# Merging the recurrence branch first, and letting another simulation set the order of the whole kernel

## Chip, cores and metric

One core of a Trainium2 chip. The metric is the device time of one execution, in microseconds (us), as the median of several runs. Engines are named as in the profile: PE is TensorE's matmul side and PEld its weight loads, DVE is VectorE, ACT ScalarE, POOL GpSimd, SP SyncE.

## The reference

The model takes 512 tokens of width 1024 through two blocks in float32. The first block mixes tokens in three branches (four heads of gated linear attention, GLA; a short convolution; eight heads of sliding-window attention), adds them with sigmoid gates, projects, and applies a gated feed-forward layer. The second block is applied twice, with its own weights for each layer. Its mixer has two branches: attention in which every query sees only the 128 keys that an index network scored highest, and a recurrence (HGRN) of four heads. The two are merged and projected:

```python
z = rmsnorm(h) @ w_in            # q, k, v, index inputs, recurrence inputs, gates
y_attn = dsa_attention(q, k, v, qi, ki, wi) @ w_attn_o
y_rec  = hgrn(f, i, ...) @ w_hgrn_o
merged = sigmoid(gate_a) * y_attn + sigmoid(gate_b) * y_rec
h = h + merged @ w_out
h = h + feed_forward(rmsnorm(h))
```

(The names are shortened; the sum over the two branches can be taken in either order.)

## The kernel before

All activations are kept with features on the partitions, as tiles of 128 x 512 (512 is the number of tokens); attention and recurrence use tiles with tokens on the partitions, NT = 4 token tiles of 128. The width 1024 makes KD = 8 feature tiles. Every large product is split into high and low parts, so that one product of a weight tile and an activation tile is three matmuls: in `project`, L193 (low weight, high activation), L194 (high weight, low activation) and L195 (high, high), each 128 x 512; in `project_tokens`, L168 to L170. A weight tile comes by DMA on SP's queue (`wraw`, three buffers), ACT casts it to `whi` (L149), and POOL or DVE subtracts it to `wlo` (L152).

The stages run in this order: a setup; the first mix (`first_mix`: GLA heads, window attention `swa`, convolution, merge of the three); the first feed-forward layer; then for each of two layers `second_mix` and `second_ffn`. `second_mix` calls `dsa` for the attention branch, then makes four recurrence heads (`hgrn_head`, which ends in `recurrence`), and merges both branches with `merge`.

In `dsa`, the string `ORDER` sets the order in which the steps are written: `x` and `X` make and rotate the index inputs, `1` to `3` are `select` (four score matmuls L874, then sixteen rounds of DVE's L885 maximum and L886 replacement), `k` and `K` make and rotate the keys, `q` and `Q` the queries (one `Q` for each block of 128 queries), `v` the values, `h` the recurrence's values, and `a` to `d` are the four blocks of queries, `attend(0)` to `attend(3)`, with one to four key blocks each. The rotations scale `aro` on DVE (L825) and transpose it on PE (L239).

A block has eight heads, each a chain: QK on PE (L925), bias and minimum on DVE (L927), exponential on ACT (L929), transposes on PE (L933), copy on ACT (L935), PV on PE (L937). After eight heads come reciprocal, scaling to `aon`, four transposes (L239) and the split into `yah` and `yal`, which the output projection of the attention branch reads. A recurrence head starts with L474, climbs seven levels in which DVE, POOL and PE take turns (L485 to L511, POOL's last step L515), and ends with state products (L397, L405, L407), an inverse square root on DVE (L229 to L233), `ron` (L415), its transposes (L239) and the split into `yhh` and `yhl`.

`merge(W, X, WO, y, acc, ahead, last)` makes `ahead` gates first, then for each of the eight output tiles one more gate, the output projection of the branch, and their product; the first branch that is merged has `acc=None` and keeps its products as the accumulator. A gate reads only the layer's input X; an output projection reads the branch's `y`, so it needs all of that branch.

PSUM has four banks for `project` ("mm"), two for the attention and two for the recurrence ("at"). Buffers of SBUF are pools: "t" (32 tiles), "i" (8), "g" (5, gates) and others.

Each engine executes its own queue in order. What order that is, the framework's scheduler decides when the kernel is built: it walks through the program and places instructions by their dependences, buffers, priorities (`tc.high_priority()` for weight loads and evictions) and its own estimate of durations. Work of the recurrence heads, gates and projections is thus placed between the steps of the attention heads, where it has no dependence on them.

Of the kernel before, what the change touches and what calls it, by code (L numbers as in the profile page):

```python
# [21 lines left out]
KD = 8  # L22
KF = 22
WARM = 12
ORDER = "xhX123kKqvQaQbQcQd"
EPS = 1e-6
NEG = -1e30
UNSEEN = -2e38
# [42 lines left out]
class Builder:  # L71
# [602 lines left out]
        self.nc.scalar.activation(g, g, AF.Tanh, scale=0.5)  # L674
        return g

    def merge(self, W, X, WO, y, acc, ahead, last):
        nc = self.nc
        G = [self.gate(W[m], X) for m in range(ahead)]
        out = []  # L680
        for m in range(KD):
            if m + ahead < KD:
                G.append(self.gate(W[m + ahead], X))
            g = G[m] if acc else self.t("acc")
            ps = self.project(WO[m], y)
            with self.tc.high_priority():
                nc.vector.scalar_tensor_tensor(g, G[m], 1.0, ps, op0=OP.add, op1=OP.mult)
            if acc:
                eng = nc.vector if last and m + ahead >= KD else nc.gpsimd
                if last and m + ahead == KD:  # L690
                    self.lows = [nc.gpsimd]
                eng.tensor_tensor(acc[m], acc[m], g, op=OP.add)
                g = acc[m]
            out.append(self.split(g, "mg") if last else g)
        return out
# [132 lines left out]
    def dsa(self, l, X):  # L828
# [61 lines left out]
        def inputs(j, name):  # L890
            got[name] = self.attention_inputs(A["w_tok"][l, j], X, name)
# [23 lines left out]
        def attend(i):  # L915
# [27 lines left out]
            for m in range(4):  # L943
# [3 lines left out]
                     q=lambda: inputs(1, "aq"), Q=rotate_query, v=values, h=gated_values)  # L947
        for c in ORDER:
            if c in steps:
# [7 lines left out]
    def second_mix(self, l, X):  # L957
        nc, A = self.nc, self.A
        W = A["w_in2"][l]
        it = iter(range(W.shape[0]))  # L960
        proj = lambda: self.project(W[next(it)], X)

        with self.on("a"):
            yattn = self.dsa(l, X)
        if self.pending:
            self.settle()
        hv = self.hv
        yh = []
        for hd in range(4):
            F = self.scaled(proj(), "hf", self.i)  # L970
            k = self.i("hk")
            nc.scalar.activation(k, F, AF.Sigmoid, scale=-1.0)
            nc.scalar.activation(F, F, AF.Sigmoid)
            if l:
                nc.gpsimd.tensor_scalar(k, k, self.om[:, hd:hd + 1], None, op0=OP.mult)
                nc.vector.tensor_scalar(F, F, self.om[:, hd:hd + 1], self.lb[:, hd:hd + 1], op0=OP.mult, op1=OP.add)
            q = self.silu2(proj(), "hq")
            v = [a[:, hd * P:(hd + 1) * P] for a in hv]
            g = self.silu2(proj(), "hg")
            yh.append(self.hgrn_head(F, q, k, v, g, self.half[:, 4 + l:5 + l], "yh"))  # L980

        acc = self.merge(A["w_gate2"][l, 0], X, A["w_po"][l, 0], yattn, None, 2, False)
        return self.merge(A["w_gate2"][l, 1], X, A["w_po"][l, 1], yh, acc, 4, True)

    def build(self, out):
        nc, A = self.nc, self.A
# [118 lines left out]
```

## Time and profile before

| | us |
|---|---|
| median of 3 runs | 2586.61 (2585.37 to 2587.36) |
| profiled run, its own time | 2592.11 |
| span of the profiled run | 2590.3 |
| PE busy | 2504.4 |
| DVE busy | 1362.4 |
| ACT busy | 1011.7 |
| POOL busy | 769.8 |

The span is the time between the first and the last instruction of one profiled execution; its mean granted clock of TensorE was 0.99. A window gives, for a stretch of this span, how long each engine was busy; the stretch less the busy time of an engine is its idle time. In a timeline row the first number is the start from the beginning of the span, the second the duration; `<-` stands between what is written and what is read, and a bracket at the end tells idle time of that engine just before, and what ended it. Matmuls overlap, so the rows of several matmuls in a row start closer together than one lasts.

### The profile page before, as it was taken

Reading aid. Unit: us, or ns where it says so; the run is one execution under the profiler, and the core shown is the slowest. Engines: PE = TensorE matmul, PEld = TensorE weight load, DVE = VectorE, ACT = ScalarE, POOL = GpSimd, SP = SyncE. Lnnn points to the kernel's source line nnn. Section 1 sums busy time; section 2 is a strip of 40 time slices with the busy share of each in tenths; the row PEclk is TensorE's granted clock in tenths of the full one; section 3 lists DMA queues with packets and bytes.
Section 4 is the critical chain, followed back from the end, with each engine's and each line's share of the span. In section 5 each row is a group of like instructions: output and inputs, shape, how many; then the busy total and the mean of one; then the engine's idle time right before and its main releaser. Section 6 shows DMA issues by size and latency. Waiting matters only on the chain.

```text
span 2590.3 us, 31616 instructions
## 1 busy us (share of the span) xinstructions
PE 2504.4 (97%) x11742; PEld 2047.2 (79%) x11742; DVE 1362.4 (53%) x2568; ACT 1011.7 (39%) x1830; POOL 769.8 (30%) x676
## 2 busy tenths in 40 slices
PE   9999999999999998899999999999798999999999
PEld 7877888888888766777888888887677788888887
DVE  4675222477764677765244444336877523444432
ACT  5633333444443344453343333334355333433322
POOL 4234334511101333643361110013465335211100
PEclk9999999999999999999999999999899999999999
DMA  4112233322233222111332223332211123222233
GB/s 136 58 60 82 87 97 98 102 98 98 97 95 96 76 74 73 42 37 59 94 99 98 97 94 95 94 98 66 73 42 40 34 96 101 96 94 96 97 108 88
DMA packets 67434, 217.66 MB, mean 84 GB/s; under 512 B 7744, under 2 KB 8640, under 8 KB 67280
## 3 DMA queue, kind: packets, MB, share of 16 engines
q1 hardware_dynamic: 67280, 215.65, 26.1%
q8 instruction: 92, 1.51, 0.2%
q14 instruction: 62, 0.51, 0.1%
HBM read 213.52 MB, written 2.10 MB: 83 GB/s over the span
## 4 chain that ended last, share of the span: by engine, by line
PE 80%; DVE 14%; POOL 3%; issue 2%; ACT 1%; DMA 0%; SPq 0%; DVEq 0%; POOLq 0%; ACTq 0%
PE mm L194 23%; PE mm L195 23%; PE mm L193 23%; DVE score L886 2%; DVE m L885 2%; PE at L925 1%; PE at L937 1%; PE at L239 1%; DVE wlo L152 1%; POOL hG L495 1%; PE mm L169 1%; PE mm L170 1%; PE mm L168 1%; DVE rsq_w L231 1%; PE at L933 1%
## 5 line engine op out<-in xcount | busy, mean ns | idle before, releaser
L149 ACT CAST whi<-wraw 128x512 fp32r<-128x512 f32 (+3 forms) x824 | 502.3, 610 | 1139.9 <-PE mm L195 950.4
L193 PE MATMUL mm<-xh,wlo 128*128 128x512 f32 x1920 | 759.0, 395 | 0.0
L194 PE MATMUL mm<-xl,whi 128*128 128x512 f32 x1920 | 758.2, 395 | 0.0
L195 PE MATMUL mm<-xh,whi 128*128 128x512 f32 x1920 | 755.5, 393 | 0.0
L152 DVE TENSOR_TENSOR wlo<-wraw,whi 128x512 fp32r<-128x512 f32 (+1 forms) x529 | 385.2, 728 | 458.5 <-ACT whi L149 455.4
L152 POOL TENSOR_TENSOR wlo<-wraw,whi 128x512 fp32r<-128x512 f32 (+2 forms) x295 | 381.4, 1293 | 760.5 <-ACT whi L149 689.6
L195 PEld LDWEIGHTS mm<-xh,whi 128*128 128x128 f32 x1920 | 361.8, 188 | 74.5 <-issue 1.9
L194 PEld LDWEIGHTS mm<-xl,whi 128*128 128x128 f32 x1920 | 361.9, 188 | 73.5 <-issue 1.7
L193 PEld LDWEIGHTS mm<-xh,wlo 128*128 128x128 f32 x1920 | 361.8, 188 | 72.9 <-issue 1.2
L193 PE MATMUL mm<-acth,wlo 128*128 128x512 f32 x528 | 205.4, 389 | 0.0
L194 PE MATMUL mm<-actl,whi 128*128 128x512 f32 x528 | 205.4, 389 | 0.0
L195 PE MATMUL mm<-acth,whi 128*128 128x512 f32 x528 | 205.4, 389 | 0.0
L733 POOL TENSOR_TENSOR fg<-fg,rstd 128x512 f32<-128x512 f32 x44 | 56.7, 1289 | 425.6 <-ACT fg L732 425.6
L168 PE MATMUL mm<-wlo,xh 128*128 128x512 f32 (+2 forms) x384 | 147.0, 383 | 17.3 <-POOL wlo L152 9.2
L169 PE MATMUL mm<-whi,xl 128*128 128x512 f32 (+2 forms) x384 | 145.2, 378 | 0.2 <-DVE xl L288 0.2
L170 PE MATMUL mm<-whi,xh 128*128 128x512 f32 (+2 forms) x384 | 145.1, 379 | 0.0
L202 DVE TENSOR_TENSOR gate<-mm,rstd 128x512 f32<-128x512 f32 x56 | 38.7, 691 | 165.2 <-PE mm L195 164.3
L277 POOL TENSOR_TENSOR acc<-acc,sq 128x512 f32<-128x512 f32 x39 | 58.9, 1509 | 199.2 <-ACT sq L274 198.3
L194 PEld LDWEIGHTS mm<-actl,whi 128*128 128x128 f32 x528 | 99.1, 188 | 20.8
L193 PEld LDWEIGHTS mm<-acth,wlo 128*128 128x128 f32 x528 | 99.1, 188 | 20.6
L195 PEld LDWEIGHTS mm<-acth,whi 128*128 128x128 f32 x528 | 99.1, 188 | 20.4
L168 PEld LDWEIGHTS mm<-wlo,xh 128*128 128x128 f32 x384 | 73.4, 191 | 36.1 <-POOL wlo L152 11.7
(352 smaller groups left out, 3333.1 us busy)
## 6 DMA issues: line engine op xcount, KB each, us to landing
wraw<-in_w_ffn_in SPq DMA_DIRECT2D x88, 512.0 KB, 3.3
wraw<-in_w_gate SPq DMA_DIRECT2D x56, 512.0 KB, 3.3
wraw<-in_w_in SPq DMA_DIRECT2D x52, 512.0 KB, 3.3
wraw<-in_w_up SPq DMA_DIRECT2D x44, 512.0 KB, 3.2
wraw<-in_w_tok SPq DMA_DIRECT2D x32, 512.0 KB, 3.2
wraw<-in_w_ffn_out SPq DMA_DIRECT2D x32, 512.0 KB, 3.6
wraw<-in_w_down SPq DMA_DIRECT2D x16, 512.0 KB, 3.6
wraw<-in_w_po SPq DMA_DIRECT2D x32, 256.0 KB, 2.6
```

The lines of the kernel that those rows point to most:

```text
L149: nc.scalar.copy(wh, raw[:, k:k + m, :])
L152: eng.tensor_tensor(wl, raw[:, k:k + m, :], wh.bitcast(F32), op=OP.subtract)
L168: nc.tensor.matmul(ps[t][:, 0:w], xh, wl, start=i == 0, stop=False)
L169: nc.tensor.matmul(ps[t][:, 0:w], xl, wh, start=False, stop=False)
L170: nc.tensor.matmul(ps[t][:, 0:w], xh, wh, start=False, stop=i == KD - 1)
L193: nc.tensor.matmul(ps, wl, xh, start=i == 0, stop=False)
L194: nc.tensor.matmul(ps, wh, xl, start=False, stop=False)
L195: nc.tensor.matmul(ps, wh, xh, start=False, stop=i == n - 1)
L277: (nc.vector if d % 2 and len(acc) > 1 else nc.gpsimd).tensor_tensor(a, a, sq, op=OP.add)
L733: nc.gpsimd.tensor_tensor(g, g, self.rstd, op=OP.mult)
L885: nc.vector.max(m8, sc[:, 0:w])
L886: nc.vector.match_replace(sc[:, 0:w], m8, sc[:, 0:w], TAKEN)
```

## The change

Four things change. In `ORDER`, two query rotations stand ahead of the first block in place of one, and the rotations for the last two blocks stand ahead of the block before, so that no rotation stands between the last two blocks. `second_mix` merges the recurrence branch first (two gates ahead) and the attention branch second (four gates ahead, as the last). `merge` gets a parameter for the pool of its accumulator, and the recurrence merge, now first, takes it from pool "i". And the program is built with `schedule_with_timeline_sim=True`: the scheduler then takes the times by which it places instructions from the toolchain's other simulation. That holds for all stages, not only for `second_mix`.

```diff
-ORDER = "xhX123kKqvQaQbQcQd"
+ORDER = "xhX123kKqvQQaQbQcd"
...
-    def merge(self, W, X, WO, y, acc, ahead, last):
+    def merge(self, W, X, WO, y, acc, ahead, last, alloc=None):
...
-            g = G[m] if acc else self.t("acc")
+            g = G[m] if acc else (alloc or self.t)("acc")
...
-        acc = self.merge(A["w_gate2"][l, 0], X, A["w_po"][l, 0], yattn, None, 2, False)
-        return self.merge(A["w_gate2"][l, 1], X, A["w_po"][l, 1], yh, acc, 4, True)
+        acc = self.merge(A["w_gate2"][l, 1], X, A["w_po"][l, 1], yh, None, 2, False, self.i)
+        return self.merge(A["w_gate2"][l, 0], X, A["w_po"][l, 0], yattn, acc, 4, True)
...
-    with tile.TileContext(nc) as tc:
+    with tile.TileContext(nc, schedule_with_timeline_sim=True) as tc:
```

The instructions stay the same in number on PE (10973), DVE (2474), POOL (681) and SP (470); ACT has 1734 instead of 1736. Their order changes on every engine. Four places of it follow; a number behind a name tells tiles of one name apart.

PE, the end of block d in layer 0, before. From the QK of the last head on, L193 to L195 with `xh` and `xl` are projections of a gate.

```order
L925 MATMUL at_8900<-kT_7952,qT_8780 128x512
L239 MATMUL at_9973<-csts_77,ron_9971 128x128 x4
L195 MATMUL mm_10023<-xh_6470,whi_10026 128x512
L193 MATMUL mm_10023<-xh_6579,wlo_10027 128x512
L194 MATMUL mm_10023<-xl_6580,whi_10026 128x512
L195 MATMUL mm_10023<-xh_6579,whi_10026 128x512
L193 MATMUL mm_10023<-xh_6688,wlo_10027 128x512
L194 MATMUL mm_10023<-xl_6689,whi_10026 128x512
L933 MATMUL at_8905<-csts_77,aL_8902 128x128 x4
L195 MATMUL mm_10023<-xh_6688,whi_10026 128x512
L193 MATMUL mm_10023<-xh_6797,wlo_10031 128x512
L194 MATMUL mm_10023<-xl_6798,whi_10030 128x512
```

The same place in the changed kernel: the last two heads and what follows.

```order
L925 MATMUL at<-kT,qT 128x512
L933 MATMUL at<-csts,aL 128x128 x4
L937 MATMUL at<-av,aPT 128x64 x4
L925 MATMUL at<-kT,qT 128x512
L933 MATMUL at<-csts,aL 128x128 x4
L937 MATMUL at<-av,aPT 128x64 x4
L239 MATMUL at<-csts,aon 128x128 x4
L193 MATMUL mm<-yah,wlo 128x512
L193 MATMUL mm<-xh,wlo 128x512
```

The gate's matmuls are gone from between the steps of a head; the same three rows (L925, L933, L937) stand six times in a row up to here, and in layer 1 five times. After the transposes of `aon` comes the first output projection of the attention branch (`yah`).

PE, the start of the fourth recurrence head in layer 0, before: L474 starts it, L488 and L509 are its levels.

```order
L925 MATMUL at_8820<-kT_7950,qT_8779 128x512
L474 MATMUL at_9845<-hq_9798,hk_9760 128x128 x4
L488 MATMUL at_9855<-lvx_9852,ones_78 128x256
L193 MATMUL mm_9985<-xh_6363,wlo_9989 128x512
L194 MATMUL mm_9985<-xl_6364,whi_9988 128x512
L195 MATMUL mm_9985<-xh_6363,whi_9988 128x512
L933 MATMUL at_8825<-csts_77,aL_8822 128x128 x4
L193 MATMUL mm_9985<-xh_6470,wlo_9989 128x512
L194 MATMUL mm_9985<-xl_6471,whi_9988 128x512
L195 MATMUL mm_9985<-xh_6470,whi_9988 128x512
L193 MATMUL mm_9985<-xh_6579,wlo_9989 128x512
L937 MATMUL at_8785<-av_8195,aPT_8830 128x64
```

In the changed kernel, a little further on in the fourth head: L509 and L464 are levels, L239 with `hG` is the transposes that follow them.

```order
L925 MATMUL at<-kT,qT 128x384
L509 MATMUL at<-lvx 112x64 x4
L509 MATMUL at<-lvx 96x64 x4
L933 MATMUL at<-csts,aL 128x128 x3
L464 MATMUL at<-lvx 64x64 x4
L937 MATMUL at<-av,aPT 128x64 x3
L925 MATMUL at<-kT,qT 128x384
L239 MATMUL at<-csts,hG 128x128 x4
L397 MATMUL at<-hv,rklT 128x128 x3
L405 MATMUL at<-hv,AT 128x128 x2
L933 MATMUL at<-csts,aL 128x128 x3
L407 MATMUL at<-rS,hf 128x128
```

Matmuls of gates stood between the levels; now only attention heads of three key blocks do. Ahead of these rows, three output sums of the recurrence merge (`yhh`) are each open on a bank, and each takes its next products when a recurrence head ends.

DVE, the key rotation in layer 0, before: L885 and L886 are rounds of the selections with three (128x384) key blocks, `aro` is what the rotation gives.

```order
L885 MAX m_7704<-score 128x8
L233 SCALAR_TENSOR_TENSOR rsq_y<-rsq_w,rsq_y 128x32
L886 MATCH_REPLACE score<-m_7704,score 128x384
L825 TENSOR_TENSOR aro<-aro,rsq_y 128x512
L885 MAX m_7707<-score 128x8
L825 TENSOR_TENSOR aro<-aro,rsq_y 128x512
L886 MATCH_REPLACE score<-m_7707,score 128x384
L825 TENSOR_TENSOR aro<-aro,rsq_y 128x512
L885 MAX m_7710<-score 128x8
L825 TENSOR_TENSOR aro<-aro,rsq_y 128x512
L886 MATCH_REPLACE score<-m_7710,score 128x384
L885 MAX m_7713<-score 128x8
```

And in the changed kernel:

```order
L233 SCALAR_TENSOR_TENSOR rsq_y<-rsq_w,rsq_y 128x32
L886 MATCH_REPLACE score<-m_7642,score 128x256
L886 MATCH_REPLACE score<-m_7668,score 128x384
L231 TENSOR_TENSOR rsq_w<-akss,rsq_y 128x32
L887 TENSOR_SCALAR score<-score 128x256
L885 MAX m_7671<-score 128x8
L232 SCALAR_TENSOR_TENSOR rsq_w<-rsq_w,rsq_y 128x32
L886 MATCH_REPLACE score<-m_7671,score 128x384
L233 SCALAR_TENSOR_TENSOR rsq_y<-rsq_w,rsq_y 128x32
L885 MAX m_7674<-score 128x8
L825 TENSOR_TENSOR aro<-aro,rsq_y 128x512 x4
L886 MATCH_REPLACE score<-m_7674,score 128x384
```

The four steps on `aro` stand together, earlier among the selection's rounds: ahead of the first, since the first selection's scores were complete, are 37 rows of L885 and L886 instead of 58. On PE, 100 matmuls of 128 x 512 stand between the last score matmul of that selection and the first key transposes instead of 152.

PE, the end of the attention and GLA heads of the first mix, in the changed kernel (L397 to L407 are state products of the last GLA head, L239 with `ron` its transposes):

```order
L397 MATMUL at<-gv,rklT 128x128 x3
L405 MATMUL at<-gv,AT 128x128 x2
L407 MATMUL at<-rS,rE 128x128
L405 MATMUL at<-gv,AT 128x128
L407 MATMUL at<-rS,rE 128x128
L405 MATMUL at<-gv,AT 128x128
L407 MATMUL at<-rS,rE 128x128
L239 MATMUL at<-csts,ron 128x128 x4
L193 MATMUL mm<-xh,wlo 128x512
```

Before, the same products of the last GLA head stood among projections of the convolution:

```order
L397 MATMUL at<-gv,rklT 128x128 x3
L405 MATMUL at<-gv,AT 128x128 x2
L194 MATMUL mm<-xl,whi 128x512
L407 MATMUL at<-rS,rE 128x128
L405 MATMUL at<-gv,AT 128x128
L407 MATMUL at<-rS,rE 128x128
L405 MATMUL at<-gv,AT 128x128
L407 MATMUL at<-rS,rE 128x128
L195 MATMUL mm<-xh,whi 128x512
L193 MATMUL mm<-xh,wlo 128x512
L194 MATMUL mm<-xl,whi 128x512
L195 MATMUL mm<-xh,whi 128x512
```

In the changed kernel no 128 x 512 matmul stands beside the last window block and the last GLA head; the projections of the convolution and all that the merge needs follow in one row.

## Rows read from the trace of the kernel before

**Rows 1.** The page: busy time and instructions of each engine; the chain by engine.

```profile
PE 2504.4 (97%) x11742; PEld 2047.2 (79%) x11742; DVE 1362.4 (53%) x2568; ACT 1011.7 (39%) x1830; POOL 769.8 (30%) x676
...
PE 80%; DVE 14%; POOL 3%; issue 2%; ACT 1%; DMA 0%; SPq 0%; DVEq 0%; POOLq 0%; ACTq 0%
```

**Rows 2.** Windows: stretch, length, busy us (count) of five engines, clock, DMA share, GB/s.

```profile
0.00:30.00 30.00, 24.22 (x97) 19.74 (x97) 18.95 (x30) 15.87 (x28) 14.07 (x13) 0.94 0.59 193
30.00:220.00 190.00, 180.75 (x1015) 149.26 (x1016) 114.91 (x317) 93.31 (x211) 62.98 (x56) 1.00 0.20 64
525.00:870.00 345.00, 345.00 (x1524) 285.67 (x1523) 234.35 (x319) 152.14 (x242) 47.46 (x34) 1.00 0.30 96
870.00:1010.00 140.00, 123.12 (x555) 97.02 (x554) 108.93 (x264) 53.12 (x110) 55.44 (x53) 0.96 0.22 72
1010.00:1212.00 202.00, 185.92 (x1084) 147.90 (x1083) 143.90 (x324) 97.92 (x201) 96.70 (x105) 1.00 0.14 44
1725.00:1860.00 135.00, 120.17 (x534) 94.82 (x533) 97.55 (x234) 51.34 (x107) 53.85 (x52) 0.94 0.22 73
1860.00:2062.00 202.00, 186.62 (x1047) 148.84 (x1046) 141.11 (x321) 95.19 (x197) 100.20 (x107) 0.95 0.13 40
```

**Rows 3.** Timeline, one head of block d: start, us, engine, line; other rows left out.

```profile
1188.28 1.08 PE L925 MATMUL at<-kT,qT 128*128 128x512 f32 x2
...
1189.40 0.69 DVE L927 CUSTOM_DVE_ANT_0 aL<-at,score 128x512 f32<-128x512 f32 x1 [0.29 <-PE at L925]
...
1190.19 0.72 ACT L929 ACTIVATE aL<-aL,anm 128x512 f32<-128x512 f32 x1 [2.22 <-DVE rsq_w L231]
...
1191.06 0.66 PE L933 MATMUL at<-csts,aL 128*128 128x128 f32 x4
...
1191.81 0.59 ACT L935 COPY aPT<-at 128x512 f32<-128x512 f32 x1 [0.18 <-PE at L933]
...
1192.48 1.07 PE L937 MATMUL at<-av,aPT 128*128 128x64 f32 x8
...
1193.39 1.08 PE L925 MATMUL at<-kT,qT 128*128 128x512 f32 x2
```

**Rows 4.** Timeline of DVE and POOL, and a window: one recurrence head.

```profile
1165.21 0.42 DVE L485 TENSOR_TENSOR lvx<-hf,hq 128x256 f32<-128x256 f32 x1
...
1179.04 1.54 POOL L515 TENSOR_TENSOR hG<-hG,hk 128x512 f32<-128x512 f32 x1
...
1193.26 0.69 DVE L415 TENSOR_TENSOR ron<-at,rsq_y 128x512 f32<-128x512 f32 x1
...
1165.50:1194.30 28.80, 27.95 (x182) 22.10 (x181) 23.34 (x52) 9.86 (x20) 14.76 (x16) 1.00 0.08 24
```

**Rows 5.** Timeline at the key rotation of layer 0.

```profile
979.08 1.26 DVE L825 TENSOR_TENSOR aro<-aro,rsq_y 128x512 f32<-128x512 f32 x1
...
980.40 0.90 PE L239 MATMUL at<-csts,aro 128*128 128x128 f32 x3 [8.27 <-DVE aro L825]
```

**Rows 6.** Groups by line on DVE, selection with three key blocks: busy, mean ns, idle.

```profile
L885 DVE MAX8 m<-score 128x8 f32<-128x384 f32 x32 | 17.7, 553 | 0.3
L886 DVE MATCH_REPLACE8 score<-m,score 128x384 f32<-128x384 f32 x32 | 17.3, 540 | 0.0
```

**Rows 7.** Timeline of PE in the first mix.

```profile
133.84 0.61 PE L582 MATMUL at<-csts,sL 128*128 128x128 f32 x4
...
135.22 1.01 PE L588 MATMUL at<-skv,sPT 128*128 128x64 f32 x8
...
211.64 0.39 PE L407 MATMUL at<-rS,rE 128*128 128x128 f32 x2
...
216.89 0.66 PE L239 MATMUL at<-csts,ron 128*128 128x128 f32 x4 [0.28 <-DVE ron L415]
```

**Rows 8.** Windows after the key wait and between the first heads.

```profile
976.20:986.40 10.20, 6.00 (x20) 4.95 (x21) 10.17 (x25) 2.94 (x13) 3.60 (x3) 0.50 0.16 54
1016.90:1023.10 6.20, 3.99 (x18) 2.77 (x19) 4.41 (x11) 3.00 (x6) 0.45 (x1) 1.00 0.00 0
```

## The prediction

> **What bounds the kernel now.** I read the engine line of the page first: PE is busy for 2504.4 of 2590.3 us, so 85.9 us is left in which it has nothing at all, and the chain that ends last is PE for 80% and DVE for 14% [rows 1]. So TensorE bounds the kernel, and a change of order can only win or lose PE's idle time, its slow clock, or both. Next I read the windows by stage, to see where that idle time lies. The feed-forward stretch 525 to 870 has none, and its 1524 matmuls of 345.00 us give 0.2264 us for one 128x512 matmul in a dense row; I call such a one a wide matmul, and use it as the unit of fill. The idle time is window less PE busy: 9.25 us in the first mix (30 to 220), 16.9 in the tokens and keys of layer 0 (870 to 1010), 16.1 in its attention and recurrence (1010 to 1212), 14.8 and 15.4 in the same two stretches of layer 1 [rows 2]. That is 72 of the 85.9, and all the places that the change reorders.
>
> Then the timeline of one attention head with four key blocks, to see what a head costs when nothing fills it [rows 3]. QK starts at 1188.28 and ends at 1189.36; the transposes (L933) start only at 1191.06, after DVE's bias and minimum and ACT's exponential: 1.70 us. They end at 1191.72 and PV (L937) starts at 1192.48, after ACT's copy: 0.76 us. The next QK starts at 1193.39, so the head takes 5.11 us, of which 2.46 us must be filled by other matmuls. In this head twelve wide matmuls stood there (12 x 0.2264 = 2.72 us), so PE never stopped.
>
> Doing the same for a recurrence head: its first DVE step (L485) is at 1165.21, POOL's last level step (L515) ends at 1180.58, and `ron` (L415) is at 1193.26, 28.05 us in all; in 1165.50 to 1194.30 PE was busy for 27.95 of 28.80 us [rows 4]. So the head ran behind full cover, and its own chain is 28 us at most. The level part, 15.4 us of POOL and DVE taking turns, hardly shortens; the 12.7 us after it hold some waits behind other heads, and I estimate 24 us for the chain by itself.
>
> Of TensorE the Trainium skill (Trainium Kernel Development and Optimization, Reading a trace) says that matmul busy time is a bad measure of headroom and weight-load busy a good one. By that measure the dense stretch stands at 285.67 / 345.00 = 82.8% [rows 2] against 2047.2 / 2590.3 = 79.0% for the whole [rows 1], an estimate of 118 us to win at most in place of 86; the sum below does not use it.
>
> **The change part by part.** The instruction counts of PE, DVE, POOL and SP stay what they were, and ACT has two table loads fewer; everything is order.
>
> *Merge order.* Before, only recurrence projections and two gates could run under the attention heads, since the merges began with the attention's output. Now the recurrence merge (its gates and output projections) and four attention gates need no attention output, so they can run there. Counting the wide matmuls in the new order between one QK and the next over the 32 heads of a layer, there are 672 where there were 311. That is more fill than is needed, but it is spent early: the first ten heads and those about the end of block c and the start of block d have 19 to 70 each, where about 12 do. The last six heads of layer 0 and the last five of layer 1 have none (first pair of excerpts). Each such head loses the 2.46 us of [rows 3]: 6 x 2.46 = 14.8, and 5 x 2.46 = 12.3. After the last PV come reciprocal, scaling, transposes and the split before the first `yah` product; only a single gate stands ready, so I add 2.2 us (0.76 and 1.5, the size of one such DVE and ACT pair in [rows 3]). Tails: 17.0 and 14.5 us.
>
> *The middle.* From the 13th to the 20th head there are only 24 wide matmuls (layer 0) and 21 (layer 1), because three of the four PSUM banks for projections hold output sums of the recurrence merge that wait for `yh` of the later recurrence heads. The third and fourth recurrence heads lie there. From L474 to the transposes of `ron` the new order puts 30 and 9 wide matmuls on PE: 6.8 and 2.0 us. Taking the 29 wide matmuls of the head in [rows 4] from its 27.95 us leaves 21.4, which hold five full-width attention heads of 5.11 - 2.46 = 2.65 us, so about 8 to 9 us for the recurrence's own matmuls. The four or so narrower heads beside each (two and three key blocks, estimates 1.3 and 1.8 us) make about 21 and 18 us of PE work. Against a chain of 24 to 28 us that leaves 9 to 17 us idle in the two heads together. PE takes its queue in order, so a wait for one chain also holds up the other; but the fill before it runs densely. I take 12 us per layer, with 4 and 18 as bounds.
>
> With 1 us for the heads that are nearly covered, layer 0 has 17.0 + 12 + 1 = 30 us of idle time in place of 16.1, **+13.9**; layer 1 has 14.5 + 12 + 1 = 27.5 in place of 15.4, **+12.1**.
>
> *Tokens and keys.* Before, PE waited 8.27 us at 980.40 for `aro` [rows 5]: DVE works through the selections (L885, L886) ahead of the key rotation. In the new order 37 of these stand between the first selection's end and the first `aro` instead of 58 (third pair of excerpts): 21 x 0.547 = 11.5 us less DVE work [rows 6]. But PE comes earlier too: 100 wide token matmuls instead of 152 lie between the last score matmul of that selection and the key transposes, 52 x 0.2264 = 11.8 us less. So the wait stays within a few us of 8. It isn't free behind it: two queries are rotated before the first block now, with 30 such DVE steps ahead instead of 24 (+3.3 us, plus the second rotation's own products of some 1 us each, as in [rows 5]) and 9 wide matmuls fewer (-2.0). I put a new wait of 4 to 5 us there, and 3 to 4 us saved at the keys and at the norm's broadcast ahead of them, which now has more token matmuls beside it. Net **+1** per layer, bounds -8 (the wait at the keys goes) and +6 (both waits stand).
>
> *First mix.* The whole program is scheduled anew, so the first mix moves too. Its last window block and last GLA head now run with no wide matmul beside them, while more than a thousand stand behind in one row (fourth pair); before, there was fill to the end. What this costs: from the last state product (ends 212.03) to the transposes of `ron` (216.89) 4.9 us; four transposes-copy-PV steps, each with the 0.77 us from 134.45 to 135.22, 3.1 us [rows 7]; eight score reductions ahead of the first exponential, some 4 us by the 0.69 us of [rows 3] less overlap; 1 us for the rest: 13 us. Against that most of the 9.25 us of [rows 2] goes, since the stages ahead are filled. **+4**, bounds -4 and +10.
>
> *Start.* Two mask casts move ahead of two splits on DVE in the first 30 us, where PE is idle for 5.8 [rows 2]: **+1**, bounds -1 and +3.
>
> *Clock.* After the wait of 8.27 us at the keys, the granted clock of 976.20 to 986.40 is 0.50, which is 1.2 GHz; yet in 1016.90 to 1023.10, where PE is busy 3.99 of 6.20 us, it stays at 1.00 [rows 8]. So gaps of 1 to 2 us with heads between them kept the full clock here, and one long wait did not. The bare heads are of the first kind; they go on for longer, however. I allow **+3** for two or three short stretches. The Trainium skill (TensorE: Matmul & The Clock Gate, A second HAM failure mode: psum-queue depth-cycling) says that PE idling briefly between matmul groups often enough makes the clock oscillate, at a cost to throughput. [rows 8] shows no drop in the shorter stretch; a rival below takes the other side.
>
> The merges, feed-forward stages and norms had no idle time and their rows stay as they were: 0, because wide matmuls cover every load there.
>
> **Sum.** 1 + 4 + 2 x 1 + 13.9 + 12.1 + 3 = +36 us. The profiled run took 2592.11 us (span 2590.3, and 1.8 around it), 5.5 above the median of the runs; 2592.1 + 36 = 2628.1 there, and 2628.1 - 5.5 = **2622.6** as a median; I say 2622.
>
> **Rivals.**
> 1. *DVE is what matters, and it is freed.* If the new order brings DVE's results so much earlier that the key wait goes in both layers (8.27 us and about 3 us for the 6.00 busy us at half clock [rows 5, 8], so -11.3 each in place of +1) and that the recurrence chains in the middle take 20 us or less (12 us each to 0), the sum is 36 - 2 x 12.3 - 2 x 12 = -12.6: about 2574. It decides once the key wait is under 2 us and both late recurrence heads take less than their PE work. For it: DVE is busy 108.93 of 140 and 143.90 of 202 us there [rows 2]. Against it: the levels of a recurrence head are 15.4 us of POOL and DVE in turns whatever the order [rows 4], and the bare heads cost 2.46 each in any case. Chance 0.18.
> 2. *The clock falls in the bare stretches.* All three PE steps of a bare head are on its chain; at 1.2 GHz their 2.65 us double, +2.65 for each of eleven heads, 29 us, and 3 to 6 more in the first mix: about 2655. For it: the 0.50 after the key wait. Against it: the 1.00 at 1016.90 [rows 8]. Chance 0.17.
> 3. *It does nothing that counts.* The order differs from end to end, but idle time moves from one place to another and the sum stays within 5 us, because the middle is covered (4 us) and the first mix wins 4: about 2587 to 2592. Chance 0.09.
>
> **How the numbers follow.** The forecast, 2597 to 2645, has 0.56. A measurement here can tell about 0.2% (5 us) from no change. Slower by more: 0.56 + 0.17 = 0.73; within: 0.09; faster by more: 0.18. The range leaves out about one in ten at each side: 2572, just beyond rival 1, to 2656, at rival 2.
>
> **What would show it.** In the changed kernel the last six and five heads of block d should come 5.1 us apart with PE about half busy; the third and fourth recurrence heads 24 to 28 us long with several us of PE waiting; a PE wait of 5 us or more both at the keys and at the first query; some 13 us of PE idle just ahead of the convolution's projections; and merges as dense as before. I am wrong if the bare heads come closer than 4.5 us, if the middle shows PE dense, or if the key waits vanish.

## The result, and the profile after

The changed kernel takes 2674.19 us (median; 2670.45 to 2675.81) against 2586.99 us for the kernel before in the same runs: a ratio of 1.0335, with a 95% interval of 1.0322 to 1.0348. It is 87 us slower. The forecast was 2622 us, with a range up to 2656: the sign was right and the size far too small.

The profiled execution has a span of 2672.2 us. The page's busy times and the chain by engine, as in [rows 1]:

```profile
PE 2543.9 (95%) x11742; PEld 2086.8 (78%) x11742; DVE 1374.0 (51%) x2568; ACT 1008.4 (38%) x1828; POOL 780.0 (29%) x676
...
PE 83%; DVE 10%; issue 3%; ACT 2%; POOL 1%; DMA 1%; SPq 0%; DVEq 0%; POOLq 0%; ACTq 0%
```

PE executes the same 11742 instructions, yet it is busy 39.5 us longer than in [rows 1] (2543.9 against 2504.4), and idle 42.4 us longer (2672.2 - 2543.9 = 128.3 against 85.9). The two make up the 81.9 us between the spans. The mean granted clock fell from 0.990 to 0.968. As the clock has two levels here, 1.00 and 0.50 (2.4 and 1.2 GHz), this is an estimated 171 us at the lower one (2 x 0.032 x 2672.2) in place of 52, and PE's steps last about twice as long there (the tail below). So about half of the loss is idle time, and the other half is put down to the clock, for which the forecast had set 3 us.

The windows of the changed kernel, with the columns of [rows 2] (stretch, length, busy us of PE, PEld, DVE, ACT and POOL, then the granted clock). The attention and recurrence of each layer are cut in four: the early heads, the stretch of the late recurrence heads, the filled heads behind it, and the bare tail.

```profile
0.00:30.00 30.00, 21.09 (x85) 17.35 (x86) 20.23 (x37) 15.43 (x27) 13.44 (x13) 0.93 0.51 175
30.00:236.00 206.00, 194.70 (x1062) 164.79 (x1060) 109.62 (x308) 98.16 (x218) 68.06 (x58) 0.97 0.20 67
883.00:1029.00 146.00, 131.30 (x581) 105.19 (x580) 110.37 (x258) 57.79 (x118) 62.71 (x60) 0.94 0.22 75
1029.00:1150.00 121.00, 111.36 (x577) 92.13 (x576) 81.19 (x168) 53.71 (x96) 58.42 (x60) 0.96 0.18 62
1150.00:1240.00 90.00, 74.85 (x421) 60.15 (x420) 58.62 (x135) 28.91 (x68) 40.34 (x43) 0.92 0.10 30
1240.00:1294.00 54.00, 54.00 (x255) 43.91 (x253) 15.80 (x31) 19.56 (x39) 14.11 (x11) 1.00 0.26 87
1294.00:1340.00 46.00, 29.53 (x103) 18.44 (x103) 7.93 (x23) 10.79 (x25) 1.27 (x1) 0.63 0.03 9
1781.00:1920.00 139.00, 124.27 (x575) 100.84 (x574) 101.66 (x230) 56.94 (x117) 62.26 (x61) 0.96 0.23 79
1920.00:2040.00 120.00, 113.32 (x585) 94.03 (x585) 85.46 (x172) 51.98 (x95) 65.72 (x65) 0.96 0.19 64
2040.00:2130.00 90.00, 77.40 (x418) 62.38 (x417) 58.96 (x137) 28.70 (x68) 39.84 (x43) 0.89 0.08 27
2130.00:2180.00 50.00, 50.00 (x239) 40.87 (x237) 14.09 (x27) 18.76 (x36) 13.76 (x12) 1.00 0.27 85
2180.00:2230.00 50.00, 36.00 (x131) 24.02 (x131) 7.64 (x20) 11.65 (x26) 2.09 (x3) 0.66 0.05 16
```

Stretch less PE busy is the idle time, in us:

| stretch | before | after | difference | forecast |
|---|---|---|---|---|
| start, first 30 us | 5.8 | 8.9 | +3.1 | +1 |
| first mix | 9.25 | 11.3 | +2.0 | +4 |
| tokens and keys, layer 0 | 16.9 | 14.7 | -2.2 | +1 |
| attention, layer 0 | 16.1 | 9.6 + 15.1 + 0 + 16.5 = 41.3 | +25.2 | +13.9 |
| tokens and keys, layer 1 | 14.8 | 14.7 | -0.1 | +1 |
| attention, layer 1 | 15.4 | 6.7 + 12.6 + 0 + 14.0 = 33.3 | +17.9 | +12.1 |

The six differences sum to +45.9; the other stretches together lost 3.5 us of idle time. The clock column shows the rest: 0.63 and 0.66 in the two tails, 0.92 and 0.89 beside the late recurrence heads, 0.96 in the early heads; [rows 2] had 1.00 and 0.95 for the two attentions as wholes. By the same estimate the two tails hold 34 us each at 1.2 GHz, so some 100 of the 171 us lie elsewhere.

How the tail of layer 0 looks in PE's timeline (QK L925, transposes L933, PV L937; nothing else stands between them):

```profile
1300.78 1.08 PE L925 MATMUL at<-kT,qT 128*128 128x512 f32 x2
1303.50 0.65 PE L933 MATMUL at<-csts,aL 128*128 128x128 f32 x4 [1.64 <-ACT aL L929]
1304.83 1.14 PE L937 MATMUL at<-av,aPT 128*128 128x64 f32 x8 [0.68 <-ACT aPT L935]
1305.77 2.01 PE L925 MATMUL at<-kT,qT 128*128 128x512 f32 x2
1309.42 1.11 PE L933 MATMUL at<-csts,aL 128*128 128x128 f32 x4 [1.64 <-ACT aL L929]
1311.26 1.97 PE L937 MATMUL at<-av,aPT 128*128 128x64 f32 x8 [0.73 <-ACT aPT L935]
1313.03 2.02 PE L925 MATMUL at<-kT,qT 128*128 128x512 f32 x2
...
1320.40 2.02 PE L925 MATMUL at<-kT,qT 128*128 128x512 f32 x2
```

The head that starts at 1300.78 takes 4.99 us, and PE waits 1.64 us in it for the exponential, close to the 1.70 that [rows 3] give. Then the clock falls: QK lasts 2.01 us instead of 1.08, PV 1.97 instead of 1.14, the waits stay, and the next heads come 7.26 and 7.37 us apart. The head at 1305.77 is the third of six bare ones; the two ahead of it, from 1295.79 on, take 4.99 us each. In layer 1 the clock falls one head sooner, within the QK of the second of five:

```profile
2187.82 1.08 PE L925 MATMUL at<-kT,qT 128*128 128x512 f32 x2
...
2192.81 1.59 PE L925 MATMUL at<-kT,qT 128*128 128x512 f32 x2
```

The longest waits of PE over the whole program:

```profile
PE at L933 <- ACT aL L929: 26.3, 21, 1.7
PE mm L168 <- DVE wlo L152: 24.1, 5, 9.7
PE at L937 <- ACT aPT L935: 12.7, 19, 0.8
...
PE at L239 <- DVE ron L415: 4.4, 1, 4.4
```

The waits for the exponential and for the copy ahead of PV, 26.3 and 12.7 us, are the bare heads, mostly those of the tails. Of the wait at the token matmuls (L168), 8.4 us lie in the tokens and keys of layer 0 and 11.2 in those of layer 1; this is what became of the key stall. In [rows 5] PE waited at the transposes of `aro`, now it waits for a weight's low part that DVE subtracts behind the selections and the rotation. The same wait in layer 0, with DVE's step:

```profile
978.31 1.80 DVE L152 TENSOR_TENSOR wlo<-wraw,whi 128x512 fp32r<-128x512 f32 x1
...
980.16 0.79 PE L168 MATMUL mm<-wlo,xh 128*128 128x512 f32 x1 [6.99 <-DVE wlo L152]
```

### The profile page after: what moved, and what is told of

It reads as the page before. It is cut to its first block, busy times and chain, and to the rows that moved or that the text cites. A ratio compares the mean times of both kernels' runs of the same rounds, so it can differ in the third digit from the quotient of the medians.

```text
span 2672.2 us, 31532 instructions
## 1 busy us (share of the span) xinstructions
PE 2543.9 (95%) x11742; PEld 2086.8 (78%) x11742; DVE 1374.0 (51%) x2568; ACT 1008.4 (38%) x1828; POOL 780.0 (29%) x676
## 4 chain that ended last, share of the span: by engine, by line
PE 83%; DVE 10%; issue 3%; ACT 2%; POOL 1%; DMA 1%; SPq 0%; DVEq 0%; POOLq 0%; ACTq 0%
PE mm L193 23%; PE mm L194 23%; PE mm L195 23%; PE mm L168 2%; PE mm L169 2%; PE mm L170 2%; DVE score L886 1%; DVE m L885 1%; PE at L937 1%; PE at L925 1%; PE at L933 1%; DVE hf L497 1%; PE at L239 1%; DVE wlo L152 1%; POOL hG L495 1%
## 5 line engine op out<-in xcount | busy, mean ns | idle before, releaser
L193 PE MATMUL mm<-xh,wlo 128*128 128x512 f32 x1920 | 762.6, 397 | 6.8 <-DVE wlo L152 3.0
L195 PE MATMUL mm<-xh,whi 128*128 128x512 f32 x1920 | 757.3, 395 | 0.0
L152 DVE TENSOR_TENSOR wlo<-wraw,whi 128x512 fp32r<-128x512 f32 (+1 forms) x529 | 392.7, 742 | 514.6 <-ACT whi L149 511.4
L193 PEld LDWEIGHTS mm<-xh,wlo 128*128 128x128 f32 x1920 | 364.4, 190 | 87.3 <-DVE wlo L152 4.9
L195 PEld LDWEIGHTS mm<-xh,whi 128*128 128x128 f32 x1920 | 363.8, 189 | 76.3 <-issue 1.0
L193 PE MATMUL mm<-acth,wlo 128*128 128x512 f32 x528 | 205.4, 389 | 0.0
L195 PE MATMUL mm<-acth,whi 128*128 128x512 f32 x528 | 205.4, 389 | 0.0
L168 PE MATMUL mm<-wlo,xh 128*128 128x512 f32 (+2 forms) x384 | 149.3, 394 | 33.3 <-DVE wlo L152 24.1
L170 PE MATMUL mm<-whi,xh 128*128 128x512 f32 (+2 forms) x384 | 146.8, 382 | 0.0
L195 PEld LDWEIGHTS mm<-acth,whi 128*128 128x128 f32 x528 | 99.1, 188 | 20.7
L168 PEld LDWEIGHTS mm<-wlo,xh 128*128 128x128 f32 x384 | 74.9, 195 | 51.6 <-DVE wlo L152 25.9
L193 PEld LDWEIGHTS mm<-acth,wlo 128*128 128x128 f32 x528 | 99.1, 188 | 20.5
```

The source lines that it names most:

```text
L152: eng.tensor_tensor(wl, raw[:, k:k + m, :], wh.bitcast(F32), op=OP.subtract)
L168: nc.tensor.matmul(ps[t][:, 0:w], xh, wl, start=i == 0, stop=False)
L170: nc.tensor.matmul(ps[t][:, 0:w], xh, wh, start=False, stop=i == KD - 1)
L193: nc.tensor.matmul(ps, wl, xh, start=i == 0, stop=False)
L195: nc.tensor.matmul(ps, wh, xh, start=False, stop=i == n - 1)
```

## Experiments

What was in doubt: which of the four edits costs; whether the clock falls because of the bare heads; and whether it matters that the fill is *spent early* (theory A), or whether the flag's order or the merge order would cost wherever the fill stood (rivals B). This table gives the wide matmuls between one QK and the next in layer 0, summed over the heads of each block, with the number of heads that have fewer than 3. The last head isn't counted, since the count ends at its QK. (Layer 1 is much the same, except that the changed kernel has 147 and 114 in blocks c and d there.)

| kernel | block a | b | c | d (to the last QK) | heads with fewer than 3 | median us |
|---|---|---|---|---|---|---|
| before | 102 | 64 | 87 | 58 | 1 | 2587 to 2590 |
| changed | 306 | 105 | 194 | 67 | 9 | 2674.2 |
| e1_no_flag, e3_order_only | 101 | 65 | 74 | 60 | 1 | 2584.0, 2584.9 |
| e2_flag_only | 306 | 30 | 0 | 0 | 21 | 2726.4 |
| e6_pace | 192 | 172 | 101 | 207 | 2 | 2669.2 |
| e7_pace_old_merge | 119 | 73 | 72 | 72 | 13 | 2731.1 |
| e8_even | 168 | 144 | 144 | 138 | 0 | 2627.9 |
| e9_even_old_merge | 93 | 81 | 78 | 72 | 0 | 2640.6 |
| e10_even2 | 168 | 144 | 143 | 127 | 0 | 2584.3 |

**Which edit.** Three kernels undo or isolate parts.

```diff
e1_no_flag (from the changed kernel)
-    with tile.TileContext(nc, schedule_with_timeline_sim=True) as tc:
+    with tile.TileContext(nc) as tc:
e4_merge_only: e1_no_flag with the old step order
+ORDER = "xhX123kKqvQaQbQcQd"
e3_order_only: the kernel before with the new step order
+ORDER = "xhX123kKqvQQaQbQcd"
```

> The changed kernel with the old scheduler's times: the new step order of the attention and the merge order stay, schedule_with_timeline_sim is left out. On PE the number of wide matmuls under the 32 heads of a layer then goes back to about 310, spread as in the kernel before. Theory A (the whole loss comes from what the other simulation makes of the order): within 8 us of the kernel before, 2579 to 2595. Rival B (the merge order or the early query rotations cost something by themselves, for instance a late recurrence head ahead of the first merge): 15 to 40 us slower than before.

> The kernel before with the two merges exchanged (recurrence first, two gates ahead, accumulator from pool i; attention second, four gates ahead) and nothing else. PE's order under the attention heads is then that of the kernel before, head by head. Theory A: 2582 to 2592, no change. Rival B: the recurrence merge waits for the fourth recurrence head, or the merge now last ends with a longer tail: slower by 5 to 20 us.

> The kernel before with the new step order alone (two query rotations ahead of the first block, the last one a block earlier). e1_no_flag has this and the merge order and came out 0.2% below before, e4_merge_only has the merge order alone and came out level. Theory A (the small gain is the step order's: query rotations no longer stand right before the blocks that need them): 2580 to 2587, as e1_no_flag. Rival B (it needs both): 2587 to 2592.

Measured: e1_no_flag 2583.95 us (ratio to before 0.9980, 0.9971 to 0.9989), e4_merge_only 2588.12 (1.0005, 0.9996 to 1.0014), e3_order_only 2584.92 (0.9983, 0.9973 to 0.9993). Theory A in all three: without the flag, the merge order changes nothing, and the step order gains about 0.2%, with an interval that just leaves out no change. The merge order does nothing by itself: under the old scheduler's times the fill of e4_merge_only is that of before in every head, and that of e1_no_flag that of e3_order_only. The attention windows of e1_no_flag have 13.2 us of idle time each (202.00 less PE busy), with the clock at 0.98:

```profile
1010.00:1212.00 202.00, 188.78 (x1082) 151.18 (x1083) 138.57 (x323) 97.59 (x202) 94.41 (x103) 0.98 0.14 45
1860.00:2062.00 202.00, 188.77 (x1081) 150.73 (x1082) 138.39 (x322) 97.11 (x201) 100.91 (x106) 0.98 0.14 44
```

**The flag without the merge order.**

```diff
e2_flag_only (from the kernel before)
-    with tile.TileContext(nc) as tc:
+    with tile.TileContext(nc, schedule_with_timeline_sim=True) as tc:
```

> The kernel before with schedule_with_timeline_sim alone: old merge order, old step order. The other simulation spends the fill that there is (recurrence projections and one gate) under the first ten heads and leaves 22 heads of each layer bare. Theory A: the merge order is what the flag needs, so this is slower than the changed kernel; 14 bare heads more (8 of them beside recurrence heads) at about 2.4 us of idle time give some 25 us per layer, and a clock at 1.2 GHz through the last dozen heads some 15 more: about 2750, at any rate over 2710. Rival B (the merge order is what costs, the flag alone is mild): below 2674.

Measured: 2726.35 us (ratio 1.0535, 1.0512 to 1.0558); expected was about 2750, or over 2710. Rival B falls: the flag is what costs, and the two new orders together make it milder. The flag with only one of them was not run; that it is the merge order is argued from the amount of fill, 672 wide matmuls in place of 336. Here the last 22 heads of layer 0 (the last one, which the table leaves out, among them) have no fill at all, the late ones not even a recurrence head beside them, and two windows laid over the late rows of both layers show the granted clock at 0.50, which is 1.2 GHz, for 74 and 87 us on end:

```profile
1211.00:1285.00 74.00, 48.08 (x140) 28.90 (x140) 12.53 (x36) 15.41 (x36) 1.26 (x1) 0.50 0.01 2
2116.00:2203.00 87.00, 57.76 (x171) 35.51 (x171) 14.17 (x39) 18.40 (x43) 2.98 (x2) 0.50 0.00 0
```

**Is it the bare heads that bring the clock down?** Work is added, in time in which TensorE had waited.

```diff
e5_fill (from the changed kernel, in attend)
                 pt = self.at([P, NT, P])
+                if i == 3 and hd >= 2:
+                    xh = X[0][0]
+                    for _ in range(4):
+                        nc.tensor.matmul(pt.rearrange("p n c -> p (n c)"), xh[:, 0:P], xh, start=True, stop=True)
```

> The changed kernel with work added: in heads 3 to 8 of block d, four 128x512 matmuls of X tiles are written to the bank of the transposes just before them (the transposes overwrite them), so that TensorE is busy for about 0.9 us more of each bare head's 5 us, in time in which it had waited for the exponential. The order of all else is the same in layer 0 and nearly so in layer 1. Theory A (the two stretches of 34 us at 1.2 GHz that begin in the bare heads come of TensorE's being half idle there): these stretches vanish or shrink, and although matmuls were added the time falls by 30 to 45 us, to 2630 to 2645. Rival B (the clock falls for another reason, or the heads are slow for their chain alone): 2672 to 2685, with heads still about 7 us apart at the end.

Measured: 2654.93 us, 19.3 less than the changed kernel, although 48 matmuls were added. PE's timeline at the same heads (L935 is the added work, L937 now the transposes, L941 PV):

```profile
1301.71 1.08 PE L925 MATMUL at<-kT,qT 128*128 128x512 f32 x2
1303.58 1.20 PE L935 MATMUL at<-xh 128*128 128x512 f32 x4 [0.79 <-DVE anm L927]
1304.62 0.60 PE L937 MATMUL at<-csts,aL 128*128 128x128 f32 x4
1305.89 1.10 PE L941 MATMUL at<-av,aPT 128*128 128x64 f32 x8 [0.68 <-ACT aPT L939]
1306.84 1.08 PE L925 MATMUL at<-kT,qT 128*128 128x512 f32 x2
```

The window of these heads in e5_fill:

```profile
1294.00:1332.00 38.00, 26.60 (x132) 17.80 (x131) 8.03 (x23) 11.11 (x25) 1.27 (x1) 0.98 0.04 11
```

And the same 38 us in the changed kernel:

```profile
1294.00:1332.00 38.00, 23.49 (x83) 13.82 (x83) 4.73 (x14) 9.14 (x20) 1.27 (x1) 0.65 0.04 10
```

The heads come 5.13 us apart; the granted clock is 0.98 against 0.65. So the bare heads do bring the clock down: a head at 1.2 GHz takes 7.37 us, a bare one at 2.4 GHz 4.99, a topped-up one 5.13. The mechanism came out as theory A had it; the expected saving of 30 to 45 us was too large. A slow head gives back 7.37 - 5.13 = 2.24 us, as the chain and its waits stay, and about four slow heads in each tail make 18 us, near the 19.3 measured. This mends the tails alone: the mean granted clock of e5_fill is 0.980, in place of 0.968 and of 0.990 before.

**Does it matter where the fill stands?** The first attempt delayed the weight loads.

```diff
e6_pace (from the changed kernel; e7_pace_old_merge: the same with the old merge order, 10 in place of 21)
+            if self.pace is not None:
+                self.filled += 3 * n
+                j = (self.filled - 72) // 21
+                if 0 <= j < 32:
+                    nc.sync.dma_start(raw[0:1, 0, 0:1], self.pace[0:1, j:j + 1])
...
+                nc.scalar.copy(self.beats[:, 8 * i + hd:8 * i + hd + 1], den[:, hd:hd + 1])
```

> The changed kernel (merge order, step order and flag as they are) with its fill held back: the sums of the exponentials of the 32 heads of a layer are copied to a small tile, and the weight load of a recurrence projection, a gate or an output projection first waits, by a transfer of 4 bytes from that tile, for the head by which its turn has come (21 wide matmuls per head, 72 ahead). The same 672 wide matmuls then stand under the heads, but 12 to 36 under nearly each, and none of the last heads is bare; heads 17 to 23, beside the third and fourth recurrence heads, have 2 to 12. Theory A (the loss is that the fill is spent early, which leaves bare heads with 2.5 us of idle time each and a slow clock): the idle time of the two tails (16.5 and 14.0 us) and most of the slow clock go, a part of the middle stays, and the time falls by 60 to 100 us, to 2575 to 2615. Rival B (the chains and PE's in-order queue cost this wherever the fill stands, or waiting weight loads cost as much): 2640 or more.

> As e6_pace, but with the old merge order (attention first), so that only some 336 wide matmuls per layer can run under the heads; they are held back to 10 per head (72 ahead), which comes out as 12 or 24 under every second or third head and none under the others. It differs from e2_flag_only by the pace and the new step order. Theory A (the place of the fill matters as much as its amount): far below the 2726 of e2_flag_only, but above e6_pace, since half of the heads are still bare singly: 2600 to 2640. Rival B (single bare heads between filled ones cost as much as a row of bare heads): above 2660.

Measured: 2669.17 us (ratio 1.0311) and 2731.14 (1.0550). By the letter rival B holds twice, although in e6_pace only two heads of layer 0 have fewer than 3 wide matmuls. The trace of e6_pace shows why this is no clean verdict on the fill (timeline of ACT and PE; L156 is the weight cast, L936 the exponential, L941 the transposes):

```profile
1036.89 1.14 ACT L156 CAST whi<-wraw 128x512 fp32r<-128x512 f32 x2 [3.56 <-DMA wraw<-in_w_in]
...
1038.05 1.28 ACT L936 ACT_TABLE_LOAD   x1
...
1039.34 0.40 ACT L936 ACTIVATE aL<-aL,anm 128x128 f32<-128x128 f32 x1
...
1039.89 0.48 PE L941 MATMUL at<-csts,aL 128*128 128x128 f32 x1 [6.89 <-ACT aL L936]
```

The weight arrives late, its cast stands ahead of the exponential in ACT's queue and waits for it, and the exponential comes when the cast and a table load are through: PE waits 6.89 us for a head that has nothing to do with that weight. The delay of loads brought waits of its own, as the rival's second half said. This wait and its like in layer 1 (6.28 us) are 13 of the 133 us that PE is idle in e6_pace; the others were not taken apart, so the question stayed open. The next kernels tie only the order on PE, with no wait and no instruction more; the order on the other engines moves with it.

```diff
e8_even (from the changed kernel; e9_even_old_merge: the same with the old merge order, 10 and 36 in place of 18 and 48)
+                with self.turn():
+                    nc.tensor.matmul(ps, wl, xh, start=i == 0, stop=False)
...
+            j = (self.filled - 48) // 18
+            self.filled += 3
+        if 0 <= j < 32:
+            with self.tc.issue_after(self.pace[j]):
+                yield
e10_even2 (from e8_even)
-            j = (self.filled - 48) // 18
+            j, m = divmod(self.filled - 48, 18)
+            j = 2 * j + (m >= 12)
...
```

`filled` counts the wide matmuls so far, and `pace` holds the QK of each head (in e10_even2 also its transposes); `issue_after` puts what follows behind that instruction in PE's queue.

> The changed kernel with the same instructions and no wait added; only their order on PE is tied down: each group of three wide matmuls of the recurrence projections, gates and output projections is queued behind the QK of the head by which its turn has come, 18 wide matmuls per head. The order on PE then has 12 to 18 of them under nearly every head of both layers (42 under the first, 30 under two), and no bare head. e6_pace wanted the same by delaying weight loads, which put late weight casts ahead of the exponentials on ACT; this does without. Theory A (the changed kernel loses because its fill is spent early): the idle time of the tails (16.5 and 14.0 us), most of that beside the late recurrence heads, and most of the slow clock go: 2585 to 2620. Rival B (the flag's order costs in each head, wherever the fill stands): 2640 or more.

> The same tie for the old merge order (attention first) with the flag and the new step order: the 312 or so wide matmuls that can run under the heads then stand 9 to 12 under every head, instead of 25 to 60 under each of the first nine and none under the other 22 as in e2_flag_only (2726). About 11 are needed to cover the 2.46 us of a head. Theory A: 2595 to 2630, a hundred us below e2_flag_only. Rival B: 2680 or more.

Measured: e8_even 2627.94 us (ratio 1.0150, 1.0135 to 1.0165), 46 less than the changed kernel; e9_even_old_merge 2640.58 (1.0196, 1.0179 to 1.0213), 86 less than e2_flag_only, from which it also differs by the step order. Both lie between the ranges of the two theories, nearer to theory A's: 8 and 11 us above its upper ends, and 12 and 39 below the lower ends of rival B. What was left shows in e8_even's waits; L953 is PV there:

```profile
PE at L953 <- ACT aPT L951: 22.9, 30, 1.7
```

All tied matmuls stood in the first gap of a head and none in the second, and PE paid the second gap 30 times.

> e8_even with each head's 18 wide matmuls tied in two portions: 12 behind its QK, where 1.70 us are to be filled, and 6 behind its transposes, where 0.76 us are. In e8_even all stood behind QK and PE still waited 22.9 us, 30 times, for the copy before PV. Theory A (idle time is decided gap by gap, by whether fill stands in that gap of PE's queue): these 23 us go nearly all and 2600 to 2612 is left. Rival B (PE is late for another chain anyway, so that the wait comes back elsewhere): 2620 or more.

Measured: 2584.28 us (ratio 0.9977, 0.9967 to 0.9986): 90 us below the changed kernel, with the same instructions (but four table loads fewer on ACT), the same flag, the same merge and step order, and 5 us below before. That is more than the 2600 to 2612 expected. The same two waits in e10_even2 (L170 is the token matmul, L955 PV):

```profile
PE mm L170 <- DVE wlo L154: 22.2, 5, 8.1
...
PE at L955 <- ACT aPT L953: 3.5, 4, 1.3
```

PV's wait fell from 22.9 to 3.5 us, and PE's busy time from 2514.6 to 2499.9 us. The line of e10_even2's page:

```profile
PE 2499.9 (97%) x11742; PEld 2061.5 (80%) x11742; DVE 1371.6 (53%) x2568; ACT 1000.1 (39%) x1824; POOL 776.5 (30%) x676
```

And its attention windows of layer 0:

```profile
1029.00:1150.00 121.00, 111.76 (x620) 93.27 (x619) 91.20 (x196) 54.01 (x108) 66.73 (x72) 0.96 0.16 55
1150.00:1240.00 90.00, 83.52 (x470) 66.76 (x470) 55.79 (x126) 33.89 (x75) 34.12 (x34) 1.00 0.15 45
1240.00:1290.00 50.00, 50.00 (x250) 40.50 (x249) 15.12 (x32) 19.11 (x38) 11.73 (x10) 1.00 0.24 77
1290.00:1330.00 40.00, 40.00 (x178) 33.09 (x178) 16.13 (x24) 15.26 (x26) 18.70 (x15) 1.00 0.33 106
```

Idle in these are 9.2, 6.5, 0 and 0 us, in place of 9.6, 15.1, 0 and 16.5. The heads of block d, which run from 1226 to 1282 here, are dense at full clock, and PE's busy time of 2499.9 us is below that of [rows 1]. The wait at the token matmuls and that for `ron` in the first mix stay much as in the changed kernel (22.2 and 4.4 us). So the loss of the changed kernel is a matter of where the fill stands in PE's queue, gap by gap. Why the flag spends it early was not tested. The orders show only that it put 25 to 60 wide matmuls under each of the first heads, 5.7 to 13.6 us of PE time, where a head has 2.46 us to fill; that it reckons with longer latencies of a head than the chip has is a guess from this.

## Why the prediction was right or wrong

**Sign and place: right.** The tails and the middle were read from the order and the head's timeline, and they came as costed: 16.5 and 14.0 us of idle time in the tails (forecast 17.0 and 14.5), 15.1 and 12.6 beside the late recurrence heads (forecast 12, bounds 4 and 18). In layer 0 the third recurrence head took 30 us from its first matmul (L474) to the transposes of `ron`, and the fourth about as long, a little more than the 24 to 28 expected:

```profile
1156.21 1.16 PE L474 MATMUL at<-hq,hk 128*128 128x128 f32 x8 [0.62 <-DVE hq L668]
...
1186.58 0.60 PE L239 MATMUL at<-csts,ron 128*128 128x128 f32 x4
```

**The clock: the step that failed.** The sum allowed +3 us "for two or three short stretches"; PE's busy time rose by 39.5 us. The step behind it took one stretch of 6.2 us at full clock [rows 8] as a sign that gaps of 1 to 2 us between heads keep the clock. That stretch holds a single gap, and wide matmuls stand on both sides of it, eleven in a row before it:

```profile
1022.06 0.33 PE L933 MATMUL at<-csts,aL 128*128 128x128 f32 x1 [2.21 <-ACT aL L929]
```

The bare heads of a tail come in a row, with two gaps each and no fill, which the text said ("they go on for longer") and did not price: in layer 0 two of them ran at 2.4 GHz and at the third the clock fell to 1.2, in layer 1 at the second. The rows on hand had a sign of it: [rows 2] gives 0.95 for the attention of layer 1 before the change, by the two levels some 20 us at 1.2 GHz, and the sum did not use it. That the clock falls in the bare stretches was rival 2, with a chance of 0.17. Its price per head was right (2.65 us forecast, 7.37 - 4.99 = 2.4 measured), but its place was too narrow: e5_fill, which mends the two tails alone, gives back 19.3 us, and the clock column shows more slow time in the recurrence stretches, the early heads and the first mix. What brings the clock down in these was not tested by itself; in e10_even2 the late recurrence heads of layer 0 run at 1.00, and the mean is 0.987. The Trainium skill's account that was weighed there (TensorE: Matmul & The Clock Gate, A second HAM failure mode: psum-queue depth-cycling: in a bf16 kernel, frequent brief idling between matmul groups makes the clock oscillate) speaks for rival 2. The tails at 0.63 and 0.66 agree that such idling brings the clock down; they show no oscillation, since it fell once in each and stayed at 1.2 GHz for the rest of the row.

**The early heads: mis-sized.** "1 us for the heads that are nearly covered" was 9.6 and 6.7 us. The count of wide matmuls between QKs was taken as cover, but PE's queue also holds the levels of the recurrence heads and the transposes of `aon`, and PE waits at these although the heads around them have 25 wide matmuls and more. The longest waits of 1029 to 1150:

```profile
PE at L509 <- DVE AT L511: 2.3, 2, 1.5
PE at L239 <- DVE aon L941: 2.2, 1, 2.2
PE at L464 <- DVE AT L511: 2.0, 1, 2.0
```

With the tails and the middle as forecast, this makes most of the difference between +26 and +43 us of idle time in the two attentions. e10_even2 has 9.2 us in the same stretch, so it isn't there that the even fill wins.

**The tokens and keys: right in size, wrong in mechanism.** Forecast was +1 per layer; -2.2 and -0.1 were measured. The wait at the keys did not stay at `aro`, nor did the query rotation show 4 to 5 us. PE now waits at L168 behind the same DVE work, up to 7.0 us in layer 0 and 9.7 in layer 1.

**First mix and start: fair.** +2.0 and +3.1 in place of +4 and +1. The longest wait in the tail of the first mix is 4.4 us at the transposes of `ron` (last line of the waits of the whole program), which stood at 4.9 in the sum; the clock is at 0.97 in that stretch, which was not in the sum. At the start, PE now waits 4.6 us at L168 for a weight's low part.

**The rivals.** Rival 1 (DVE is freed) failed at both its conditions: the wait behind the selections is still there at its new place, up to 9.7 us, and the third recurrence head took 30 us. Rival 3 (nothing that counts) fell with the result.

## What to carry to other kernels

Fill counts by the gap, not by the sum: work that covers a chain has to stand in each of the chain's waits in the in-order queue, and a scheduler can spend it in the wrong ones. Read the new order before believing in more available fill, count the fill in each gap, and price a row of bare gaps twice: once by the wait, and once by the clock, which here fell to half after one or two such heads and made each further one 2.4 us longer. Here, tying the order on PE (an issue-order edge, which added no instruction) took back 46 us with the fill in one gap of each head and 90 us with it in both, while delaying the loads brought new waits.

## What the runs showed of the hardware

A row of attention heads in which TensorE is busy for about 2.65 of 5 us ran at 2.4 GHz for two heads (layer 0) or one (layer 1) and then at 1.2 GHz for as long as the row went on; in e2_flag_only a window of 87 us lies wholly at 0.50. Four matmuls of 128x512 more in each head, some 0.9 us in 5.1, kept the clock at 0.98 through the same heads. With these 48 matmuls added, the kernel was 19.3 us faster.
